# Four small-vector loads queued behind the eighth token tile's load, sinks loaded as whole rows

## The chip, the cores and the metric

The kernel runs on one core of one Trainium2 chip. Times are device microseconds (us) of one execution; the number that counts is the median over several executions. A profile comes from one execution of its own, and its span runs from that execution's first recorded instruction to its last.

The engines are TensorE (PE; its weight loads are PEld), VectorE (DVE), ScalarE (ACT), GpSimd (POOL) and SyncE (SP). SP computes nothing here: it issues plain loads and stores. POOL issues the transfers that add to what lies at their destination. "SPq" marks a DMA-issuing instruction on SP's queue.

## What is computed

One layer of a hybrid encoder block on x, 1024 tokens by 1024 channels, float32:

```
h    = rmsnorm(x, norm_g)
proj = h @ w_in                    # q, k, v, za, u, vs, zs, two merge gates
a    = window_sink_attention(rope(q), rope(k), v, att_sinks)   # 16 heads of 64
a    = (a * silu(za)) @ w_att_out
v2   = layernorm(gelu(vs), sg_ln_g, sg_ln_b)
sg   = gelu(u) * (masked sg_w per 128-token block @ v2 + sg_b)
sg   = (sg * silu(zs)) @ w_sg_out
y    = sigmoid(gate_a + b_merge[0]) * a + sigmoid(gate_s + b_merge[1]) * sg
out  = rmsnorm(x + y @ w_o, final_g)
```

The small vectors of this case are `att_sinks` (16 numbers, one per head), `b_merge` (2 x 1024, laid out 128 x 16), `sg_ln_g` and `sg_ln_b` (1024 each, laid out 128 x 8).

## The kernel before, in words

**Products.** Every float32 product is made of three products of a high and a low part in TensorE's fp32r format: high by high, high by low, low by high. `split` (L170 on) makes a high part with an ACT cast (L177) and a low part with a DVE subtraction (L178). The large products take two row blocks and two column blocks at a time and use seven block products in the place of eight (`gemm_pair`, `product` at L396).

**The head** is the first stage, to about 101 us. Tokens come in eight tiles of 128 rows. `normed_tile(t)` (L669) does for tile t, in this order: `load_x(t)` (L571, the DMA at L575) into one of the three `wr` buffers that `raw_tile` (L94) hands out in turn; `scale_of` (L633): an ACT Square of the tile with its row sums (L648), then the inverse root, made of one ACT Sqrt (L148) and four small DVE instructions (L150 to L155); `scaled_part` (L651): for each half of 512 channels one DVE scaling in place (L654) and four TensorE transposes into a PSUM bank (L659); `cast_part` (L663): an ACT cast to the high part (L665) and a DVE subtraction to the low part (L666); and an ACT copy of the transposed half (L678). The second transposes of a tile are the last readers of its `wr` buffer, so they free it. Tiles 0, 1 and 2 are loaded and normalised in `first_tiles` (L743). Then a loop runs (L842):

```python
for t in range(5):
    if t > 1:
        vs_gemm(t)
    if t + 3 < NT:
        normed_tile(t + 3)
```

`vs_gemm(t)` (L710, products at L682) multiplies tile t by half of the `vs` weights. At t = 3 the loop also calls `of_chain` twice (weights that POOL adds up in place, `s` tiles) and `ask(6)` (L829): a plain load of weight tile 6 into a `wr` buffer. At t = 4 it loads and adds up `apart`, calls `ask(7)`, and `of_raw` (L838) casts and splits what `ask(6)` brought, at L177 and L178. After the loop comes a block whose order on PE, ACT and DVE is written by hand; it begins with four `plain` weights (L901), the third of which is the one of `ask(6)`, the fourth that of `ask(7)`.

The buffers decide when a load can be issued. Tile 3 takes tile 0's `wr` buffer, tile 4 that of tile 1, and so on: tile 5 waits for tile 2, tile 6 for tile 3, `ask(6)` for tile 4, tile 7 for tile 5, `ask(7)` for tile 6.

**Order of instructions.** Outside the hand-ordered blocks a scheduler orders each engine's instructions when the program is built. Each engine then runs its own list strictly in that order, and an instruction that waits holds up all those behind it on its engine. `after(second, first)` (L180) only puts `second` behind `first` in an engine's list; it adds no wait at run time. SP's transfers go to one hardware queue, POOL's to another.

**Small vectors.** The sinks are loaded by two DMAs of 64 partitions (L1028), 4 runs of 2 numbers (8 bytes) in each partition, so that head pair c of parity e lies in columns 2c and 2c+1 of the half e; both stand behind tile 4's load in SP's list. `bm_sb`, `lg_sb` and `lb_sb` are loaded by L1032 to L1034 with no order given. `nsink_sb` is the negated `sink_sb` (L1139). First readers: `lb_sb` and `lg_sb` at 112.8 and 115.0 us (L1092, L1111), `sink_sb` at 189.5 (L1139), `bm_sb` at 680.7 (L1910).

Of the kernel before, what the change touches and what calls it, by code (L numbers as in the profile page):

```python
# [25 lines left out]
F32 = mybir.dt.float32  # L26
# [6 lines left out]
P = 128  # L33
# [4 lines left out]
NT = S // P  # L38
# [16 lines left out]
def hybrid_tile(  # L55
# [16 lines left out]
    nc = tc.nc  # L72

    dram = ctx.enter_context(tc.tile_pool(name="dram", bufs=1, space=bass.MemoryType.DRAM))
    const = ctx.enter_context(tc.tile_pool(name="const", bufs=1))
# [5 lines left out]
    def nm(s):  # L81
        count[0] += 1
        return f"{s}_{count[0]}"
# [4 lines left out]
    def mtile(shape, dt, tag, bufs, pool=None):  # L88
        return (pool or main).tile(shape, dt, name=nm(tag), tag=tag, bufs=bufs)
# [4 lines left out]
    def raw_tile():  # L94
        return mtile([P, D], F32, "wr", 3)
# [20 lines left out]
    make_identity(nc, ident[:])  # L116
    warm = const.tile([P, 1], F32, name="warm")

    sink_sb = const.tile([P, 8], F32, name="sink_sb")
    nsink_sb = const.tile([P, 8], F32, name="nsink_sb")  # L120
    bm_sb = const.tile([P, 16], F32, name="bm_sb")
    lg_sb = const.tile([P, KC], F32, name="lg_sb")
    lb_sb = const.tile([P, KC], F32, name="lb_sb")
# [56 lines left out]
    def after(second, first):  # L180

        tc.add_manual_dep(
            second.ins,
            first.ins.name,
            mybir.DependencyInfo(mybir.DependencyClass.NoSync, mybir.DependencyReason.DATA),
            reason="order",
        )
# [5 lines left out]
    def slot(name, shape=(P, 4, HALF), dt=F32R):  # L193

        return mtile(list(shape), dt, "T_" + name, 1)

    def new_b(names=FORMS):
        return {n: (slot(n + "h"), slot(n + "l")) for n in names}
# [26 lines left out]
    def add_to(dst, src):  # L225
        return nc.gpsimd.dma_start(dst, src, accum_op=ALU.add)

    def copy_to(dst, src):
        nc.sync.dma_start(dst, src)
# [150 lines left out]
    term = [None]  # L380
# [188 lines left out]
    x_loads = {}  # L569

    def load_x(t, parts=1):  # L571
        xt = raw_tile()
        for c in range(parts):
            cs = slice(c * D // parts, (c + 1) * D // parts)
            x_loads[t] = nc.sync.dma_start(xt[:, cs], x[t * P : (t + 1) * P, cs])  # L575
        return xt
# [8 lines left out]
    x_in = {0: load_x(0, 2)}  # L585
# [7 lines left out]
    def keep_busy(n):  # L593
        return [
            nc.tensor.matmul(idle[:], ones_b[:, 0:P], ones_b[:], start=True, stop=True) for _ in range(n)
        ]
# [3 lines left out]
    behind = keep_busy(7)[-1]  # L600
    for j in range(4):
        for i in range(2):
# [8 lines left out]
            behind = spread  # L611
# [7 lines left out]
    f = {n: slot(at, dt=F32) for n, at in (("f11", "t3l"), ("f21", "t4l"))}  # L619
# [13 lines left out]
    def scale_of(t, vector=False):  # L633
        xt = x_in[t] if t in x_in else load_x(t)
        if t == 0:
            s0, s1, base, half_base = (stat() for _ in range(4))
            for c, ss in enumerate((s0, s1)):
                nc.scalar.activation(junk[:, half_of(c)], xt[:, half_of(c)], AF.Square, accum_out=ss[:])
            nc.vector.tensor_scalar(base[:], s0[:], 1.0 / D, EPS, op0=ALU.mult, op1=ALU.add)
            nc.vector.tensor_scalar_mul(half_base[:], base[:], -0.5)  # L640
            return xt, rstd_of(s1[:], 1.0 / D, (base[:], half_base[:]))
        ss = stat()
        if vector:
            squares[t] = nc.vector.scalar_tensor_tensor(
                junk[:], xt[:], 1.0, xt[:], op0=ALU.mult, op1=ALU.mult, accum_out=ss[:]
            )
        else:
            squares[t] = nc.scalar.activation(junk[:], xt[:], AF.Square, accum_out=ss[:])  # L648
        return xt, rstd_of(ss[:], 1.0 / D)

    def scaled_part(t, j, xt, r):  # L651
        cs = half_of(j)
        gain = g_in[j][:] if t < 2 else g_sb[:, cs]
        scale = nc.vector.scalar_tensor_tensor(xt[:, cs], xt[:, cs], r[:], gain, op0=ALU.mult, op1=ALU.mult)  # L654
        scalings.append(scale)
        pt = bank("o" if t == 1 else "tp")
        for i in range(4):
            k = j * 4 + i
            turn = nc.tensor.transpose(pt[:, i * P : (i + 1) * P], xt[:, k * P : (k + 1) * P], ident[:])  # L659
        p3 = pt[:].rearrange("p (k c) -> p k c", k=4)  # L660
        return p3, (f[f"f{j + 1}{t // 4 + 1}"][:, :, tokens(t)], p3), scale, turn

    def cast_part(t, j, p3):  # L663
        hi, lo = quarter_of(t, j)
        casts.append(nc.scalar.copy(hi, p3))  # L665
        los.append(nc.vector.tensor_sub(lo, p3, hi.bitcast(F32)))  # L666
        return casts[-1], los[-1]

    def normed_tile(t, scale=None):  # L669
        xt, r = scale or scale_of(t)  # L670
        if t == 4:
            hb.update(new_b(("b22",)))
            f.update((n, slot(at, dt=F32)) for n, at in (("f12", "t4h"), ("f22", "t3h")))
        for j in range(2):
            p3, copy, _, _ = scaled_part(t, j, xt, r)
            if t <= 4 or j:
                cast_part(t, j, p3)
            nc.scalar.copy(*copy)  # L678
# [31 lines left out]
    def vs_gemm(t, middle=None):  # L710

        acc = vs_acc[t] = bank("o" if t in (2, 3) else "mm")[:]
        part = acc
        if t == 1:
            vs_acc["p1"] = bank("sc")[:]
        dst = xh[:, t, 0:HALF]
        for k in range(KC):
            if middle and k in middle:
                middle[k]()
            if t < 4 and k == 4:  # L720
                nc.scalar.copy(dst, acc)
                part = vs_acc["p1"]
            pace[0] = vs_step(part, t, k, *vs_w[k], (0, KC - 1) if t == 4 else (k & 4, k | 3))
            if t == 4 and k in (0, 4):
                part_of_early(1)
        if t == 4:
            nc.scalar.copy(dst, acc)
        else:
            nc.vector.tensor_add(dst, dst, part)
# [91 lines left out]
    def of_chain(c, nxt=None):  # L821
        raw = chain[c] if c < 2 else apart
        weights.append(vs_weights(raw[:]))
        if nxt is not None:
            add_to(raw[:], w[W_VS + nxt])
# [3 lines left out]
    def ask(first, second=None, raw=None):  # L829
        raw = raw or raw_tile()  # L830
        copy_to(raw[:], w[W_VS + first])
        if second is not None:
            add_to(raw[:], w[W_VS + second])
        waiting.append(raw)
# [3 lines left out]
    def of_raw():  # L838
        weights.append(vs_weights(waiting.pop(0)[:]))

    first_tiles()
    for t in range(5):  # L842
        if t > 1:
            vs_gemm(t)
        if t + 3 < NT:
            normed_tile(t + 3)
        if t == 2:
            for c in range(2):
                chain.append(mtile([P, D], F32, "s", 2))
                copy_to(chain[c][:], w[W_VS + 4 + c])  # L850
        if t == 3:
            for c in range(2):
                of_chain(c, 6 + c)
            ask(6)
        if t == 4:
            copy_to(apart[:], w[W_VS + 4])
            add_to(apart[:], w[W_VS + 6])
            add_to(apart[:], w[W_VS])
            ask(7)
            of_raw()  # L860
# [162 lines left out]
    for t in (0, 4):  # L1023
        nc.vector.tensor_scalar_mul(mv[:, t, 1:2], mv[:, t, 1:2], 1.0 / D)
    nc.vector.tensor_scalar_mul(mv[:, 5:8, 1], mv[:, 5:8, 1], 1.0 / D)
    sinks_by = sinks.rearrange("(c e r) -> e c r", e=2, r=2)
    for e in range(2):
        later = nc.sync.dma_start(  # L1028
            sink_sb[e * 64 : (e + 1) * 64].rearrange("p (c r) -> p c r", r=2), sinks_by[e].partition_broadcast(64)
        )  # L1030
        after(later, x_loads[4])
    nc.sync.dma_start(bm_sb[:], b_merge)  # L1032
    nc.sync.dma_start(lg_sb[:], ln_g)
    nc.sync.dma_start(lb_sb[:], ln_b)  # L1034
    split_next()
    head.close()

# [98 lines left out]
    while late:  # L1136
        late.pop(0)()
    stage.close()
    after(nc.vector.tensor_scalar_mul(nsink_sb[:], sink_sb[:], -1.0), term[0])  # L1139


    stage = ExitStack()
# [622 lines left out]
    with tc.manual_schedule(engines={mybir.EngineType.PE, mybir.EngineType.Activation, mybir.EngineType.DVE}):  # L1765
        p = 0
# [297 lines left out]
    for p in range(4):  # L2064
        n, t, acc, x11 = N_PAIRS + p, T_ORDER[p], accs[p], firsts[p]
# [204 lines left out]
```

## Time and profile before

| | us |
|---|---|
| three runs: lowest, median, highest | 907.41, 909.19, 909.72 |
| the profiled execution, its time | 906.95 |
| its span | 905.2 |
| PE busy / DVE busy / ACT busy / POOL busy | 890.8 / 700.1 / 547.9 / 152.8 |
| granted TensorE clock, mean | 0.999 |

The profile has a page of totals and answers to questions on single engines, lines and stretches of time. In an answer in order of time, a row gives the start and the length in us, the engine, the line, the operation, what it writes and reads, and how many instructions are merged (x2); a bracket at the end gives how long the engine stood idle ahead of it, and what released it. In the table by stretches, each engine's busy time stands in turn (PE, PEld, DVE, ACT, POOL), then the granted clock, the mean busy share of the 16 DMA engines, and the rate in GB/s.

### The profile page before, as it was taken

Reading aid. Unit: us, or ns where it says so; the run is one execution under the profiler, and the core shown is the slowest. Engines: PE = TensorE matmul, PEld = TensorE weight load, DVE = VectorE, ACT = ScalarE, POOL = GpSimd, SP = SyncE. Lnnn points to the kernel's source line nnn. Section 1 sums busy time; section 2 is a strip of 40 time slices with the busy share of each in tenths; the row PEclk is TensorE's granted clock in tenths of the full one; section 3 lists DMA queues with packets and bytes.
Section 4 is the critical chain, followed back from the end, with each engine's and each line's share of the span. In section 5 each row is a group of like instructions: output and inputs, shape, how many; then the busy total and the mean of one; then the engine's idle time right before and its main releaser. Section 6 shows DMA issues by size and latency. Waiting matters only on the chain.

```text
span 905.2 us, 13294 instructions
## 1 busy us (share of the span) xinstructions
PE 890.8 (98%) x4269; PEld 742.3 (82%) x4269; DVE 700.1 (77%) x1256; ACT 547.9 (61%) x1098; POOL 152.8 (17%) x230
## 2 busy tenths in 40 slices
PE   8899999999999999999999999999999999999997
PEld 5678888888888888888888888888888888888886
DVE  6788876666678677888888887656698699579986
ACT  8677733334445567888778886444476385367443
POOL 2112322213011001222211111011100111210012
PEclk9999999999999999999999999999999999999999
DMA  7888998867788879999998996875568665998633
GB/s 279 210 209 196 267 191 178 178 153 232 240 276 261 276 260 321 287 249 269 250 351 266 251 236 185 302 268 185 166 211 307 216 204 177 283 323 284 204 111 122
DMA packets 131765, 213.45 MB, mean 236 GB/s; under 512 B 12940, under 2 KB 61072, under 8 KB 131696
## 3 DMA queue, kind: packets, MB, share of 16 engines
q1 hardware_dynamic: 108728, 148.89, 50.6%
q0 software_dynamic: 22672, 63.45, 29.7%
q8 instruction: 34, 0.56, 0.2%
q10 hardware_dynamic: 296, 0.27, 0.1%
q14 instruction: 35, 0.29, 0.1%
HBM read 155.80 MB, written 90.31 MB: 272 GB/s over the span
## 4 chain that ended last, share of the span: by engine, by line
PE 94%; DMA 2%; ACT 2%; DVE 1%; issue 0%; SPq 0%; ACTq 0%
PE ps_mm L396 45%; PE ps_o L396 27%; PE ps_tp L396 4%; PE ps_sc L1451 3%; PE ps_sc L396 2%; DMA wr<-in_x_dram 2%; PE ps_o L682 2%; PE ps_tp L1103 2%; PE ps_tp L1532 2%; PE ps_o L1592 2%; PE ps_mm L682 2%; PE ps_tp L682 1%; PE ps_sc L682 1%; PE ps_o L1600 1%; PE ps_tp L1542 1%; ACT wl L648 1%
## 5 line engine op out<-in xcount | busy, mean ns | idle before, releaser
L177 ACT CAST wh<-s 128x1024 fp32r<-128x1024 f32 (+1 forms) x84 | 84.4, 1006 | 78.2 <-PE ps_mm L396 27.6
L178 DVE TENSOR_TENSOR wl<-s,wh 128x1024 fp32r<-128x1024 f32 (+1 forms) x84 | 98.5, 1173 | 18.6 <-ACT wh L177 18.2
L178 DVE TENSOR_TENSOR wl<-wr,wh 128x512 fp32r<-128x512 f32 (+1 forms) x65 | 61.6, 949 | 63.2 <-ACT wh L177 61.3
L177 ACT CAST wh<-wr 128x512 fp32r<-128x512 f32 (+1 forms) x65 | 53.9, 831 | 63.8 <-PE ps_mm L396 36.3
L1492 ACT ACTIVATE pr<-ps_sc,sm 128x192 f32<-128x192 f32 (+2 forms) x128 | 51.3, 408 | 24.6 <-DVE sm L1483 21.4
L396 PE MATMUL ps_o<-T_b22h,wh 128*128 128x512 f32 x148 | 59.1, 399 | 0.0
L339 POOL DMA_DIRECT2D sums<-in_w_dram x48 | 35.5, 888 | 133.8 <-PE ps_mm L396 83.1
L396 PE MATMUL ps_o<-T_t1h,wh 128*128 128x512 f32 x148 | 58.1, 392 | 0.0
L396 PE MATMUL ps_o<-T_b22h,wl 128*128 128x512 f32 x148 | 57.9, 391 | 0.0
L396 PE MATMUL ps_o<-T_t1h,wl 128*128 128x512 f32 x148 | 57.8, 390 | 0.0
L396 PE MATMUL ps_o<-T_b22l,wh 128*128 128x512 f32 x148 | 57.8, 390 | 0.0
L396 PE MATMUL ps_o<-T_t1l,wh 128*128 128x512 f32 x148 | 57.7, 390 | 0.0
L396 PE MATMUL ps_mm<-T_t4h,wh 128*128 128x512 f32 (+1 forms) x144 | 55.9, 388 | 0.0
L396 PE MATMUL ps_mm<-T_t2h,wh 128*128 128x512 f32 x140 | 55.4, 396 | 0.0
L396 PE MATMUL ps_mm<-T_t4h,wl 128*128 128x512 f32 (+1 forms) x144 | 55.3, 384 | 0.0
L396 PE MATMUL ps_mm<-T_t4l,wh 128*128 128x512 f32 (+1 forms) x144 | 55.3, 384 | 0.0
L396 PE MATMUL ps_mm<-T_b11h,wh 128*128 128x512 f32 x140 | 55.2, 394 | 0.0
L396 PE MATMUL ps_mm<-T_t3h,wh 128*128 128x512 f32 x140 | 54.9, 392 | 0.0
L396 PE MATMUL ps_mm<-T_b11l,wh 128*128 128x512 f32 x140 | 54.7, 391 | 0.0
L396 PE MATMUL ps_mm<-T_b11h,wl 128*128 128x512 f32 x140 | 54.6, 390 | 0.0
L396 PE MATMUL ps_mm<-T_t3h,wl 128*128 128x512 f32 x140 | 54.6, 390 | 0.0
L396 PE MATMUL ps_mm<-T_t2h,wl 128*128 128x512 f32 x140 | 54.6, 390 | 0.0
(488 smaller groups left out, 2476.5 us busy)
## 6 DMA issues: line engine op xcount, KB each, us to landing
wr<-in_w_dram SPq DMA_DIRECT2D x80, 256.0 KB
sums<-in_w_dram POOLq DMA_DIRECT2D x24, 512.0 KB, 7.6
s<-sums SPq DMA_DIRECT2D x24, 512.0 KB
wr<-in_w_dram SPq DMA_DIRECT2D x17, 512.0 KB
q_hl<-qhl SPq DMA_DIRECT2D x16, 512.0 KB
q<-q_hl SPq DMA_DIRECT2D x64, 128.0 KB
y_dr<-x POOLq DMA_DIRECT2D x28, 256.0 KB, 6.3
sums<-in_w_dram POOLq DMA_DIRECT2D x24, 256.0 KB, 8.1
```

The source lines that it names most:

```text
L177: hi_casts.append(nc.scalar.copy(hi, src))
L178: return nc.vector.tensor_sub(lo, src, hi.bitcast(F32))
L339: return lambda: paced(nc.gpsimd.dma_start(dst, src, accum_op=op))
L396: mm = nc.tensor.matmul(acc, lt, rt, start=fresh and k == 0 and n == 0, stop=k == 3 and n == 2, skip_group_check=True,)
L648: squares[t] = nc.scalar.activation(junk[:], xt[:], AF.Square, accum_out=ss[:])
L682: mm = nc.tensor.matmul(acc, lt, rt, start=first and n == 0, stop=last and n == 2, skip_group_check=True)
L1103: nc.tensor.matmul(pm[:, t * P : (t + 1) * P], xh[:, half * 4 + t, g * P : (g + 1) * P], bias[-1][1][:, g % 2, :], start=True, stop=True,)
L1451: nc.tensor.matmul(sc[:, i, lo:hi], q_of[:, c, i * P : (i + 1) * P], kt[:, f, lo:hi], start=f == 0, stop=f == 1,)
L1492: nc.scalar.activation(st.pr[:, i, place_of(c, lo, hi)], st.sc[c][:, i, lo:hi], AF.Exp, bias=st.nmax[:, c, i : i + 1], scale=-1.0, accum_o ...
L1532: nc.tensor.transpose(st.inner[0:wide, at : at + P], st.pr[:, i, place_of(c, 64 if st.t else P, 192)], ident[:])
L1542: nc.tensor.transpose(st.ends[0:wide, i * P : (i + 1) * P], st.pr[:, i, P : P + wide], ident[:])
L1592: nc.tensor.matmul(st.po[:], lt, rt, start=i == 0, stop=False, skip_group_check=True)
```

## The change

Three edits.

1. At the end of the loop's pass t = 3, behind `normed_tile(6)` and ahead of `of_chain` and `ask(6)`, tile 7 is loaded. It so takes the buffer that tile 4 leaves, `ask(6)` takes tile 5's and `ask(7)` still tile 6's.
2. The four small loads are issued there too, in one chain behind tile 7's load on SP's list: `lb_sb`, `lg_sb`, `bm_sb`, `sink_rows`.
3. The sinks come as one DMA of whole rows, all 16 numbers (64 bytes) to each of 128 partitions. At the place of the old negation, three DVE copies sort them by parity: one for each half of the partitions into a scratch tile, one back; the fourth DVE instruction negates.

```diff
-    sink_sb = const.tile([P, 8], F32, name="sink_sb")
-    nsink_sb = const.tile([P, 8], F32, name="nsink_sb")
+    sink_rows = const.tile([P, 16], F32, name="sink_rows")
+    sink_sb, nsink_sb = sink_rows[:, 0:8], sink_rows[:, 8:16]
...
         if t + 3 < NT:
             normed_tile(t + 3)
+        if t == 3:
+            x_in[7] = load_x(7)
+            behind = x_loads[7]
+            for dst, src in (
+                (lb_sb, ln_b),
+                (lg_sb, ln_g),
+                (bm_sb, b_merge),
+                (sink_rows, sinks.partition_broadcast(P)),
+            ):
+                later = nc.sync.dma_start(dst[:], src)
+                after(later, behind)
+                behind = later
...
-    sinks_by = sinks.rearrange("(c e r) -> e c r", e=2, r=2)
-    for e in range(2):
-        later = nc.sync.dma_start(
-            sink_sb[e * 64 : (e + 1) * 64].rearrange("p (c r) -> p c r", r=2), sinks_by[e].partition_broadcast(64)
-        )
-        after(later, x_loads[4])
-    nc.sync.dma_start(bm_sb[:], b_merge)
-    nc.sync.dma_start(lg_sb[:], ln_g)
-    nc.sync.dma_start(lb_sb[:], ln_b)
...
-    after(nc.vector.tensor_scalar_mul(nsink_sb[:], sink_sb[:], -1.0), term[0])
+    by_half = mtile([P, NT], F32, f"st{NT}", 5)
+    behind = term[0]
+    for e in range(2):
+        half = slice(e * 64, (e + 1) * 64)
+        by_e = sink_rows[half].rearrange("p (c e r) -> p c e r", e=2, r=2)[:, :, e, :]
+        taken = nc.vector.tensor_copy(by_half[half].rearrange("p (c r) -> p c r", r=2), by_e)
+        after(taken, behind)
+        behind = taken
+    nc.vector.tensor_copy(sink_sb, by_half[:])
+    nc.vector.tensor_scalar_mul(nsink_sb, by_half[:], -1.0)
```

## The prediction, on record before the result

> **What bounds the kernel now.** I read the page first, then who makes TensorE wait, then the stretches, then the lists of the engines where it waits.
>
> ```profile
> span 905.2 us, 13294 instructions
> PE 890.8 (98%) x4269; PEld 742.3 (82%) x4269; DVE 700.1 (77%) x1256; ACT 547.9 (61%) x1098; POOL 152.8 (17%) x230
> ```
> ```profile
> PE ps_tp L659 <- DVE wr L654: 2.2, 1, 2.2
> PE ps_tp L659 <- ACT xh L727: 1.6, 1, 1.6
> PE ps_o L595 <- DVE T_b22l L106: 1.5, 1, 1.5
> PE ps_tp L659 <- issue: 0.9, 1, 0.9
> PE ps_sc L603 <- DVE wh L589: 0.9, 1, 0.9
> PE ps_mm L777 <- ACT T_t2h L700: 0.5, 1, 0.5
> ```
> ```profile
> 0.00:50.00 50.00, 42.22 (x203) 31.30 (x203) 35.84 (x78) 36.40 (x69) 10.15 (x21) 1.00 0.81 248
> 50.00:100.00 50.00, 50.00 (x224) 41.43 (x223) 40.35 (x55) 38.49 (x60) 10.52 (x17) 1.00 0.84 214
> ```
>
> TensorE is the bound. The second fence holds all its waits of the whole execution, and all lie in the head: from 50 to 100 us it is busy for 50.00 of 50.00. So whatever lets TensorE through the first 50 us sooner arrives at the end, as long as nothing behind starts to wait. Three of the waits stand at L659, the transposes of token tiles 5, 6 and 7:
>
> ```profile
> 36.97 0.63 PE L659 MATMUL ps_tp<-ident,wr 128*128 128x128 f32 x4 [2.21 <-DVE wr L654]
> 43.29 0.63 PE L659 MATMUL ps_tp<-ident,wr 128*128 128x128 f32 x4 [0.91 <-issue]
> 49.40 0.63 PE L659 MATMUL ps_tp<-ident,wr 128*128 128x128 f32 x4 [1.57 <-ACT xh L727]
> ```
>
> 2.21 + 0.91 + 1.57 = 4.69 us: all that this change can win on TensorE. (The bracket names the last releaser only; the lists below show what held it.) What feeds these tiles is SP's list:
>
> ```profile
> 10.65 0.43 SPq L1032 DMA_DIRECT2D bm_sb<-in_b_merge_dram  x1
> 11.33 0.33 SPq L1033 DMA_DIRECT2D lg_sb<-in_ln_g_dram  x1
> ...
> 17.63 0.33 SPq L575 DMA_DIRECT2D wr<-in_x_dram  x1
> 18.00 1.41 SPq L1028 DMA_DIRECT2D sink_sb<-in_sinks_dram  x2
> 19.46 0.60 SPq L1034 DMA_DIRECT2D lb_sb<-in_ln_b_dram  x1
> 21.27 0.33 SPq L575 DMA_DIRECT2D wr<-in_x_dram  x1
> ```
> ```profile
> 31.63 0.33 SPq L229 DMA_DIRECT2D wr<-in_w_dram  x1
> 38.34 0.33 SPq L575 DMA_DIRECT2D wr<-in_x_dram  x1
> 44.70 2.47 SPq L229 DMA_DIRECT2D wr<-in_w_dram  x2
> ```
> ```profile
> 21.27 10.50 DMA wr<-in_x_dram
> ...
> 38.34 6.04 DMA wr<-in_x_dram
> ```
> ```profile
> 20.00:23.00 3.00, 3.00 (x19) 2.64 (x18) 1.97 (x6) 3.00 (x7) 0.35 (x1) 1.00 0.16 52
> 23.00:26.00 3.00, 3.00 (x15) 2.23 (x14) 2.92 (x5) 3.00 (x7) 0.00 (x0) 1.00 0.27 38
> ```
>
> Tile 4 is asked for at 17.63, tile 5 at 21.27; 31.63 is `ask(6)`, 38.34 tile 7, 44.70 `ask(7)`. Tiles 5 and 7 have the same size, yet tile 5 takes 10.50 us to land and tile 7 takes 6.04. While tile 5 is under way the DMA engines are nearly idle: shares of 0.16 and 0.27. It is not short of bandwidth; it stands in SP's queue behind the sinks, whose 512 pieces of 8 bytes drain slowly, and behind `lb_sb`. ScalarE and VectorE show the rest:
>
> ```profile
> 28.84 0.59 ACT L678 COPY T_t4l<-ps_tp 128x512 f32<-128x512 f32 x1
> 31.79 1.06 ACT L648 ACTIVATE wl<-wr 128x1024 f32<-128x1024 f32 x1 [2.36 <-DMA wr<-in_x_dram]
> ...
> 36.10 1.07 ACT L648 ACTIVATE wl<-wr 128x1024 f32<-128x1024 f32 x1
> ...
> 38.31 1.05 ACT L177 CAST wh<-wr 128x1024 fp32r<-128x1024 f32 x1 [1.04 <-DMA wr<-in_w_dram]
> 39.27 0.58 ACT L678 COPY T_t4h<-ps_tp 128x512 f32<-128x512 f32 x1
> ...
> 40.22 0.30 ACT L148 ACTIVATE st<-st,eps_sb 128x1 f32<-128x1 f32 x1
> ...
> 44.41 1.06 ACT L648 ACTIVATE wl<-wr 128x1024 f32<-128x1024 f32 x1 [2.61 <-DMA wr<-in_x_dram]
> ```
>
> The Squares of tiles 5, 6 and 7 are at 31.79, 36.10 and 44.41. At 38.31 stands the cast of `ask(6)`. It comes ahead of two things that tile 6 needs: the copy of tile 5's half at 39.27 (VectorE works behind it) and tile 6's own root at 40.22. So tile 6's transposes, at 43.29, are held by the landing of a weight that is only multiplied later.
>
> **The change part by part.**
>
> *The early small loads go* (bm, lg, sinks, lb). Tile 5's issue does not move: it waits for tile 2's buffer, not for SP. It should land well inside the 6.04 us of tile 7, at 27.3 or before, ahead of the end of ScalarE's work at 28.84 + 0.59 = 29.43. Its Square then starts at 29.43 instead of 31.79, 2.36 us earlier, and its transposes can start at 36.97 - 2.36 = 34.61. TensorE runs dry at 36.97 - 2.21 = 34.76. **The wait of 2.21 goes.** What is late next is tile 6.
>
> *Tile 7 ahead of `ask(6)`.* It takes tile 4's buffer, so SP issues it at 31.63, where `ask(6)` is now; `ask(6)` moves to tile 5's release. Does tile 7 land sooner than `ask(6)` did, 38.31 - 31.63 = 6.7 us later? POOL's adds fill the engines at that time:
>
> ```profile
> 30.96 0.88 POOL L226 DMA_DIRECT2D apart<-in_w_dram  x1 [10.61 <-DMA apart<-in_w_dram]
> 31.53 2.07 POOL L226 DMA_DIRECT2D s<-in_w_dram  x2
> ```
> ```profile
> 32.00:38.00 6.00, 3.79 (x22) 2.95 (x21) 3.89 (x9) 4.90 (x10) 1.60 (x2) 1.00 0.95 203
> 38.00:42.00 4.00, 4.00 (x21) 3.31 (x19) 2.09 (x6) 2.80 (x5) 0.77 (x1) 1.00 1.05 213
> ```
>
> The engines are 0.95 busy while `ask(6)` lands. Tile 6's data is out of the queue sooner now, and POOL's adds start somewhat earlier, so I take 0 to 1 us off: tile 7 lands at 37.3 to 38.3, and I use 37.8. The Trainium skill, DMA: Bandwidth & Descriptors, Issuing engines are not separate DMA queues, says that transfers started by different engines run on the same 16 DMA engines and interleave; it speaks against gaining by asking earlier, and the two shares above agree with it.
>
> Now the wait that the change adds. Tile 7's Square is ready in ScalarE's list where the cast of `ask(6)` was: same buffer, same size, same moment of issue, and it comes from earlier in the program than the cast. I expect it in that place, behind tile 6's Square and ahead of the copy of tile 5's half. ScalarE then waits there for tile 7 as it waits now for the weight; behind it are tile 5's copies and cast and tile 6's root, and behind these VectorE's subtractions and scaling, and TensorE. The Square and its read of the sums take 0.1 us more than the cast (1.16 against 1.05). So tile 6's transposes start at 43.29 - 0.5 + 0.1 = 42.9. TensorE reaches them 2.2 us sooner than now, and waits about 2.7 us in the place of 0.91: **most of what tile 5 gave is taken back here.**
>
> *Tile 7's own wait of 1.57* goes. Its Square is done 5 us ahead of now, and the list between tile 6 and tile 7 on TensorE is the same work: 49.40 - 1.57 - 43.29 = 4.54 us from tile 6, so tile 7 starts at 42.9 + 4.54 = 47.4 in the place of 49.40.
>
> *`ask(6)` and `ask(7)` come later in the list.* `ask(6)` is issued when tile 5's transposes end, near 36.0, behind four small loads. It changes places with tile 7, whose data landed at 44.4 when asked for at 38.34; I take 42 to 45. Its cast then stands where tile 7's Square is now, ahead of the copies of tile 6's transposes, and tile 7's transposes wait for these, since they write the same PSUM banks. From landing to tile 7 that is 1.05 + 0.58 = 1.7 us if VectorE has scaled tile 7 by then, and about 4.5 if its list keeps tile 7's scaling behind tile 6's work as now (44.41 to 49.40, less a half us for the Square's sums). A landing at 42 costs nothing by either; one at 45 costs nothing by the first and 2 us by the second. I take 43 and the second: 43 + 4.5 = 47.5, 0.1 later than the 47.4 above. The multiplication itself, the third `plain` weight, follows two others and does not come into it before 50.
>
> *The small loads behind tile 7.* 512 pieces again, but of 32 and 64 bytes. No row shows this load alone; from below nothing (hidden under POOL's adds), from above the delay of the old group, 10.50 - 6.04 = 4.5 us on the transfer behind it, `ask(6)`. I take 2 us, inside the 42 to 45 above, because half the pieces are the bm and lg loads, which held up nothing that waited. Their readers come at 112 us and later.
>
> ```profile
> 189.50 0.16 DVE L1139 TENSOR_SCALAR nsink_sb<-sink_sb 128x8 f32<-128x8 f32 x1
> ...
> 196.78 0.69 DVE L283 TENSOR_TENSOR s<-wr 128x512 f32<-128x512 f32 x1 [5.09 <-DMA wr<-in_w_dram]
> ```
>
> *The sorting.* Three DVE instructions more, each like L1139's 0.16: 0.5 us at 189.5. TensorE does not wait there, and VectorE stands idle for 5.09 us soon after; cost nothing. Without that cover it would be 0.5.
>
> **Sum.** Transposes of tile 7 at 47.5 in the place of 49.40: **1.9 us gained**, 4.69 of waits becoming about 2.8. The profiled execution would go from 906.95 to 905.05, its span from 905.2 to 903.3. The median shown, 909.19, lies 2.24 above the profiled execution; from it I forecast 909.19 - 1.9 = **907.3 us**.
>
> **The rivals.**
>
> *All three waits go: 904.5.* Tile 7's Square does not hold tile 6, either because the scheduler puts it behind tile 5's copies and tile 6's root, or because tile 7 lands by 35. Then 4.69 is gained. For it: tile 5's half is transposed by 35.3, close to where ScalarE falls idle, so a small shift in the order suffices. Against it: the cast stands there today under the same conditions. The Trainium skill, DMA: Bandwidth & Descriptors, Anatomy of one DMA, gives about 2.0 us plus the bytes by 436 GB/s for one transfer; as an estimate that is 3.2 us for 512 KB, a landing at 34.8, and so this rival's time. The trace disagrees: 10.50 and 6.04 for that size.
>
> *The small loads hold `ask(6)`, slower: 912.7.* If they drain behind tile 7 as the old sinks did ahead of tile 5, and beside POOL's adds, `ask(6)` lands at 44 + 4.5 = 48.5. By the longer way above tile 7's transposes follow at 48.5 + 4.5 = 53.0, 3.5 us behind the 49.40 of now. From a landing of 43 on this eats the gain, and from 44.9 on the change loses. Against it: there are no pieces of 8 bytes any more.
>
> *No change: 909.2.* The lists fall differently: the tiles' transposes placed earlier among TensorE's products wait just as long, or `ask(6)` lands near 45.
>
> **How the numbers follow.** Forecast 0.5; all waits gone 0.25; no change 0.13; slower 0.12. The range, 903.9 to 910.0, holds the first three with a half us of scatter around them and leaves out the slower one. What a measurement of this kernel can tell from no change is about 0.3%, 2.7 us. Faster by more than that is the second case and the upper tail of the first: 0.36. Slower by more: 0.12. Within: 0.52.
>
> **What would show each step.** Right: ScalarE's Square of tile 5 directly behind the work ending at 29.4 with no wait for a DMA; DMA shares near 0.2 between 20 and 26 gone; no wait at tile 5's transposes, one of 2 to 3.5 us at tile 6's, none at tile 7's; a Square waiting for `in_x` just ahead of tile 5's copies. Wrong: tile 6's transposes before 41; a wait at `plain` weights between 46 and 60; any wait of TensorE after 60, where I have taken it that every load has time to spare.

## The result, and the profile after

| | before | changed |
|---|---|---|
| median, lowest to highest (5 runs each, side by side) | 909.72 (907.41 to 910.33) | **905.07** (904.32 to 905.66) |
| the profiled execution, its time and span | 906.95, 905.2 | 904.32, 902.5 |
| mean granted clock in it | 0.999 | 0.998 |
| TensorE's waits at L659, tiles 5, 6 and 7 | 2.21 + 0.91 + 1.57 | 0 + 1.30 + 0.96 + 0 |

The ratio is 0.9953, with a 95% interval of 0.9938 to 0.9967: faster by 0.3 to 0.6%. The page's totals after:

```profile
span 902.5 us, 13292 instructions
PE 890.4 (99%) x4269; PEld 742.5 (82%) x4269; DVE 700.3 (78%) x1259; ACT 547.5 (61%) x1098; POOL 152.7 (17%) x230
```

Every engine does what it did, three DVE instructions apart; the span lost 2.7 us, 2.4 of them waits of TensorE at L659. The first rows of the table of waits:

```profile
PE ps_o L595 <- DVE T_b22l L106: 1.5, 1, 1.5
PE ps_tp L659 <- issue: 1.3, 1, 1.3
PE ps_tp L659 <- DVE st L153: 1.0, 1, 1.0
```

TensorE's list in order of time, the transposes of tile 5, of tile 6 in two halves, and of tile 7 (x8):

```profile
34.95 0.63 PE L659 MATMUL ps_tp<-ident,wr 128*128 128x128 f32 x4
...
39.17 0.63 PE L659 MATMUL ps_tp<-ident,wr 128*128 128x128 f32 x4 [1.30 <-issue]
42.14 0.63 PE L659 MATMUL ps_tp<-ident,wr 128*128 128x128 f32 x4 [0.96 <-DVE st L153]
46.03 1.03 PE L659 MATMUL ps_tp<-ident,wr 128*128 128x128 f32 x8
```

Tiles 5 and 7 no longer wait, tile 6 waits twice. Why it does stands in ScalarE's list:

```profile
29.36 1.07 ACT L648 ACTIVATE wl<-wr 128x1024 f32<-128x1024 f32 x1
...
35.63 1.06 ACT L648 ACTIVATE wl<-wr 128x1024 f32<-128x1024 f32 x1 [1.50 <-DMA wr<-in_x_dram]
36.59 0.19 ACT L648 ACTIVATION_READ_ACCUMULATOR wl<-wr 128x1 f32 x1
36.81 0.29 ACT L148 ACTIVATE st<-st,eps_sb 128x1 f32<-128x1 f32 x1
37.01 0.56 ACT L678 COPY T_t4h<-ps_tp 128x512 f32<-128x512 f32 x1
38.99 1.06 ACT L648 ACTIVATE wl<-wr 128x1024 f32<-128x1024 f32 x1 [1.41 <-DMA wr<-in_x_dram]
39.96 0.19 ACT L648 ACTIVATION_READ_ACCUMULATOR wl<-wr 128x1 f32 x1
40.05 0.57 ACT L665 CAST T_b22h<-ps_tp 128x512 fp32r<-128x512 f32 x1
...
41.37 0.58 ACT L678 COPY T_t3h<-ps_tp 128x512 f32<-128x512 f32 x1
41.86 1.05 ACT L177 CAST wh<-wr 128x1024 fp32r<-128x1024 f32 x1
```
```profile
40.65 0.69 DVE L666 TENSOR_TENSOR T_b22l<-ps_tp,T_b22h 128x512 fp32r<-128x512 f32 x1 [0.98 <-ACT T_b22h L665]
41.26 0.74 DVE L654 SCALAR_TENSOR_TENSOR wr<-wr,st,g_sb 128x512 f32<-128x512 f32 x1
```

Tile 5's Square runs at 29.36 without a wait. Tile 6's Square, at 35.63, now waits 1.50 us for its own data: that is tile 6's first wait. Tile 7's Square, at 38.99, waits 1.41 us in front of the cast of tile 5's second half at 40.05. Two things that tile 6's second half needs stand behind that cast: on VectorE the subtraction that reads its result (40.65) and then the scaling of that half (41.26 to 42.00), and on ScalarE the copy at 41.37 that empties the PSUM bank into which that half is transposed. Both end just ahead of 42.14: the second wait. The cast of `ask(6)`, at 41.86, waits for nothing.

Tile 6 lands later than the queue in front of it would explain. The DMA engines by stretches, and POOL's adds:

```profile
20.00:23.00 3.00, 3.00 (x19) 2.63 (x18) 1.99 (x6) 3.00 (x7) 0.33 (x1) 1.00 0.80 141
23.00:26.00 3.00, 3.00 (x15) 2.22 (x13) 2.88 (x6) 3.00 (x6) 0.99 (x2) 1.00 0.82 246
```
```profile
25.01 0.88 POOL L226 DMA_DIRECT2D apart<-in_w_dram  x1 [4.69 <-DMA apart<-in_w_dram]
25.58 1.19 POOL L226 DMA_DIRECT2D s<-in_w_dram  x1
28.18 0.85 POOL L226 DMA_DIRECT2D s<-in_w_dram  x1 [1.41 <-ACT T_b21h L665]
```

Where the engines stood at 0.16 and 0.27 they are at 0.80 and 0.82: nothing clogs the queue. But the adds were held by that clog too, though they go by POOL's queue: before, the second add to `apart` waited 10.61 us for the first one to land, now 4.69. They came at 30.96 and 31.53 before and come at 25.01 to 28.18 now, beside the loads of tiles 6 and 7.

**The scatter before.** Executions of the kernel before differ among themselves by over 6 us (906.09 to 912.56), those of the changed one by less than 2. A further look at the kernel before, told among the experiments, shows another form of the same head, with one wait of 4.52 us at tile 6 and, behind it, TensorE at half its clock. Over the 83 executions of the kernel before that ran beside the experiments, 18 had a mean granted clock of 0.998 or more (median 906.92), 30 had 0.996 or 0.997 (908.45) and 35 had 0.995 or less (910.10). The changed kernel had 0.997 or more in all ten. So two things make up the gain in the median: fewer waits in like executions (2.63 us in the pair of profiles, about 2 us between the medians at a clock of 0.998 or more), and no executions of the longer form among the ten. Why `ask(6)` lands so much later in one execution than in another stays open.

### The profile page after: what moved, and what is told of

It reads as the page before. It is cut to its first block, busy times and chain, and to the rows that moved or that the text cites. A ratio compares the mean times of both kernels' runs of the same rounds, so it can differ in the third digit from the quotient of the medians.

```text
span 902.5 us, 13292 instructions
## 1 busy us (share of the span) xinstructions
PE 890.4 (99%) x4269; PEld 742.5 (82%) x4269; DVE 700.3 (78%) x1259; ACT 547.5 (61%) x1098; POOL 152.7 (17%) x230
## 4 chain that ended last, share of the span: by engine, by line
PE 97%; DMA 1%; ACT 1%; DVE 0%; SPq 0%; issue 0%; ACTq 0%
PE ps_mm L396 45%; PE ps_o L396 27%; PE ps_tp L396 4%; PE ps_sc L1463 3%; PE ps_sc L396 2%; PE ps_o L682 2%; PE ps_mm L682 2%; PE ps_sc L682 2%; PE ps_tp L1106 2%; PE ps_tp L1544 2%; PE ps_o L1604 2%; PE ps_tp L682 1%; PE ps_o L1612 1%; DMA wr<-in_x_dram 1%; PE ps_tp L1554 1%; DMA T_t3h<-in_w_dram 1%
```

## The experiments

Each gives its median beside runs of the kernel before on the same chip; that kernel's medians were 908.65, 909.61 and 908.37 us in the three sets, so the ratio compares better than the time.

### The changed kernel again

No edit, beside the first set.

> The changed kernel again, beside the three variants. Theory G (given back): tile 5's wait is gone, but POOL's adds start 6 us sooner, lie beside tiles 6 and 7 and hold their landing, so that about half of the 4.69 us of waits is kept: 2.3 to 2.7 us under the kernel before by the profiles; by the medians anything from 2.3 to 4.7. Rival S (sum of the parts): both parts add up, 4 us or more in every comparison.

904.9 us (904.21 to 905.26), ratio 0.9960 [0.9947, 0.9973]. Tile 6 waits 0.73 + 1.41 us, tiles 5 and 7 none. The gain holds: 3.6 us by the ratio, 3.75 between the medians, which fits theory G and is under the 4 us of S.

### The small loads late, tile 7 where it was

From the changed kernel (the calls of `of_chain` and `ask(6)` only move up; their old lines below, which go, are not shown):

```diff
         if t == 3:
-            x_in[7] = load_x(7)
+            for c in range(2):
+                of_chain(c, 6 + c)
+            ask(6)
+        if t == 4:
             behind = x_loads[7]
             for dst, src in (
```

> The small loads moved late and the sinks in whole rows, but tile 7 still asked for behind ask(6). G: tile 5's transposes near 34.9 with no wait to speak of, tile 6's Square waits for its data until about 35.6, the cast of ask(6) until about 39, tile 6's transposes near 44, tile 7's near 48.5 in the place of 49.40: about 0.9 us gained. S: 2.2 us gained, tile 5's whole wait.

908.44 us, ratio 0.9996 [0.9985, 1.0008]: **nothing is gained**, less than either theory said. Tile 5's wait is gone, its transposes run at 34.67. But see ScalarE, TensorE, and two stretches by windows, whose third last number is the granted clock:

```profile
40.19 1.04 ACT L177 CAST wh<-wr 128x1024 fp32r<-128x1024 f32 x1 [5.21 <-DMA wr<-in_w_dram]
```
```profile
45.16 1.09 PE L659 MATMUL ps_tp<-ident,wr 128*128 128x128 f32 x4 [5.06 <-ACT st L148]
```
```profile
42.00:45.00 3.00, 0.00 (x0) 0.00 (x0) 2.89 (x9) 2.29 (x6) 0.00 (x0) 0.64 0.06 23
45.00:50.00 5.00, 4.84 (x16) 4.14 (x17) 4.34 (x11) 1.79 (x4) 0.72 (x1) 0.53 0.28 71
```

`ask(6)` was issued at 31.50 beside adds that now came at 26.34 and 26.91. ScalarE waits 5.21 us for it, in front of tile 5's copies, and TensorE waits 5.06 us at tile 6, more than the three waits of before together (4.69). Behind it the granted clock is 0.53. The same list from tile 6's first transposes to the first `plain` product takes 50.48 - 45.16 = 5.32 us here, and 46.53 - 43.29 = 3.24 in the profile of before: 2.1 us more for the clock.

### Tile 7 first, the small loads where they were

From the kernel before:

```diff
+        if t == 3:
+            x_in[7] = load_x(7)
```

> Tile 7 asked for ahead of ask(6), the small loads as before. G: tile 5 still lands 10.5 us after its issue and its wait of 2.2 us stays; the waits at tiles 6 and 7 shrink to under 0.7 together: 1.8 to 2.5 us gained, as much as the whole change within 0.6 us. S: no more than 1.5 us gained, and at least 1 us less than the whole change.

906.89 us, ratio 0.9987 [0.9975, 0.9998]: 1.2 us gained by the ratio, 1.8 between the medians. That is well under the whole change, as theory S said. The waits in its profile:

```profile
36.69 0.63 PE L659 MATMUL ps_tp<-ident,wr 128*128 128x128 f32 x4 [1.79 <-DVE wr L654]
...
47.49 0.63 PE L659 MATMUL ps_tp<-ident,wr 128*128 128x128 f32 x4 [1.68 <-DVE wr L654]
```
```profile
44.44 1.05 ACT L177 CAST wh<-wr 128x1024 fp32r<-128x1024 f32 x1 [3.26 <-DMA wr<-in_w_dram]
```

Tile 5 waits nearly as before. Tile 6 waits for nothing. The cast of `ask(6)` lands late, ahead of tile 6's copies, and costs 1.68 us at tile 7's second half.

### The sinks as whole rows at their old place

From the kernel before, edit 3 alone (the sorting is as in the change and not shown):

```diff
-    for e in range(2):
-        later = nc.sync.dma_start(
-            sink_sb[e * 64 : (e + 1) * 64].rearrange("p (c r) -> p c r", r=2), sinks_by[e].partition_broadcast(64)
-        )
-        after(later, x_loads[4])
+    later = nc.sync.dma_start(sink_rows[:], sinks.partition_broadcast(P))
+    after(later, x_loads[4])
```

> The kernel before with the sinks as one load of whole rows, sorted later, but issued at the old place behind tile 4, and the other small loads where they were. Theory F (form: pieces of 8 bytes drain slowly): tile 5 lands by 29.4, its Square waits for no DMA and its transposes start by 35.0; the total then behaves like the variant with late small loads, no more than 1 us under the kernel before, since the cast of ask(6) holds tile 6. Rival P (place: any small load there holds tile 5): tile 5's Square still starts at 31 or later.

908.56 us, ratio 0.9997 [0.9983, 1.0012]. Tile 5's Square does not wait any more, so it was the pieces of 8 bytes and not the place that held tile 5. And again nothing is gained, by the same way as with the small loads late:

```profile
41.17 1.04 ACT L177 CAST wh<-wr 128x1024 fp32r<-128x1024 f32 x1 [2.68 <-DMA wr<-in_w_dram]
```
```profile
46.15 1.08 PE L659 MATMUL ps_tp<-ident,wr 128*128 128x128 f32 x4 [4.95 <-ACT st L148]
```

### The sinks' loads issued twice

From the kernel before, a second pair of the same loads into `nsink_sb`, which is overwritten later:

```diff
+    for dst in (sink_sb, nsink_sb):
...
+                dst[e * 64 : (e + 1) * 64].rearrange("p (c r) -> p c r", r=2), sinks_by[e].partition_broadcast(64)
```

> The kernel before, the sinks' two loads issued twice (the second copy is overwritten later). Theory F: twice 512 pieces of 8 bytes; tile 5 lands about 7 us later than now, 17 to 18 us behind its issue; the wait at its transposes grows from 2.2 to 8 to 10 us, and the clock is halved behind it in every execution: 6 to 11 us slower than the kernel before. If the pieces cost nothing: no difference within 1 us.

909.06 us, ratio 1.0005 [0.9991, 1.0019]: no slower, so theory F missed by far. Tile 5's Square waits 3.43 us. With 512 pieces it waited 2.36, 1.96 and 0.83 in three profiles (the one of before, the one with tile 7 first, and the second look below). So 512 more pieces cost some 1 to 2.6 us of that wait and not 7. One more thing moves here: `lb_sb`'s load, ahead of tile 5's before, now stands behind it. How the clog grows with the number of pieces, and what sets its length, stays open.

### A second look at the kernel before

No edit.

> The kernel before again, for its profile. If the mean granted clock is under 0.998, its timeline has a half-clock stretch of 3.4 or 6.8 us that begins within the waits at the transposes of tiles 5 to 7; if it is 0.998 or more, none there.

910.21 us, mean clock 0.994.

```profile
46.41 1.09 PE L659 MATMUL ps_tp<-ident,wr 128*128 128x128 f32 x4 [4.52 <-issue]
```
```profile
41.44 1.05 ACT L177 CAST wh<-wr 128x1024 fp32r<-128x1024 f32 x1 [4.75 <-DMA wr<-in_w_dram]
```
```profile
45.00:50.00 5.00, 3.59 (x13) 3.15 (x14) 4.31 (x10) 2.62 (x5) 0.72 (x1) 0.50 0.06 20
```

Here tile 5 waits only 0.78 us, and the late landing of `ask(6)` costs 4.52 at tile 6 with the clock at 0.50 behind, as expected at this mean clock. The same cast is in the same place as in the profile that I predicted from, where it waited 1.04.

### The adds held back

From the changed kernel, the adds to `s` made to wait for tile 6's Square, and the second add to `apart` for tile 7's; a real wait this time (`held_until(move, first)` makes `move` wait at run time until `first` is done):

```diff
-            add_to(raw[:], w[W_VS + nxt])
+            added = add_to(raw[:], w[W_VS + nxt])
+            if 6 in squares and 7 not in squares:
+                held_until(added, squares[6])
...
-            add_to(apart[:], w[W_VS])
+            held_until(add_to(apart[:], w[W_VS]), squares[7])
```

> The changed kernel, with POOL's adds to the chain tiles held until tile 6's Square and the second add to apart until tile 7's. G: tile 6 lands by 32 and tile 7 by 36; the waits at their transposes fall from 2.26 us to under 0.6: 1.7 to 2.3 us faster than the changed kernel. S, or if another traffic delays tile 6: no difference within 0.5 us. Slower if the chain tiles come too late for their casts at 52.6 and 55.6.

906.26 us, ratio 0.9973 [0.9963, 0.9983]: not faster than the changed kernel (0.9960), where theory G expected 1.7 to 2.3 us. But the Squares of tiles 6 and 7 run at 34.80 and 36.80 with no wait for data: it was the adds that made tiles 6 and 7 late. Then the adds, at 36.27 and 39.63, meet `ask(6)`:

```profile
43.90 1.05 ACT L177 CAST wh<-wr 128x1024 fp32r<-128x1024 f32 x1 [3.76 <-DMA wr<-in_w_dram]
```
```profile
46.95 0.76 PE L667 MATMUL ps_tp<-ident,wr 128*128 128x128 f32 x4 [2.15 <-DVE wr L662]
```

### The adds held until the weight is cast

From the changed kernel, the same three adds made to wait for the cast of `ask(6)`.

```diff
-                of_chain(c, 6 + c)
+                of_chain(c)
...
-            add_to(apart[:], w[W_VS])
...
+            for c in range(2):
+                held_until(add_to(chain[c][:], w[W_VS + 6 + c]), hi_casts[-1])
+            held_until(add_to(apart[:], w[W_VS]), hi_casts[-1])
```

> The changed kernel with POOL's adds to the chain tiles and the second one to apart held until the cast of ask(6). Theory G: tiles 6, 7 and ask(6) each land beside little other traffic, the Squares and the cast wait for nothing, all waits at the transposes together under 0.5 us, no half-clock stretch in the head: 1.8 to 2.3 us faster than the changed kernel. If the chain tiles now come too late, waits appear between 52 and 62 and it is no faster.

906.18 us, ratio 0.9969 [0.9956, 0.9983]: again no faster than the changed kernel. No transposes wait, and tile 7's run at 44.09, 1.9 us ahead of the changed kernel's. That is lost again between 65 and 76 us, later than expected, where products wait, most of them for weights that the adds make (the last row is another wait):

```profile
PE ps_mm L690 <- DVE wl L178: 1.5, 2, 0.8
...
PE ps_mm L690 <- ACT wh L177: 0.4, 1, 0.4
PE ps_mm L690 <- ACT xh L960: 0.3, 1, 0.3
```

### The wait filled with products

From the kernel with the small loads late and tile 7 at its old place; the tiles' transposes are pinned near where they stood:

```diff
+        if t == 4:
+            for _ in range(4):
+                nc.tensor.matmul(acc, ident[:], g_sb[:, 0:HALF], start=True, stop=True)
...
+            if t == 4 and k == 3:
+                after(turns[6], pace[0])
...
+                if (c, t, k) == (0, 0, 0):
+                    after(turns[7], pace[0])
```

> The kernel with the small loads late and tile 7 at its old place (e1, 908.44 us), with four extra float32 products of the identity by the gains (128x512) put on TensorE ahead of the t = 4 products, and the transposes of tiles 6 and 7 pinned within two or three products of where they stood. They write a PSUM bank that the next product overwrites, so nothing that is computed changes. By the transposes' 0.16 us for 128 columns they take 2.6 to 3.4 us, inside the 5.06 us that TensorE waits at tile 6 there: the wait becomes about 2, and TensorE arrives at the same moment. Theory C (what e1 lost beyond its waits is the half clock that follows a wait of about 5 us): the stretch at half clock from 42.83 to 49.66 goes, the mean clock is 0.996 or more in nearly all executions, and the median falls by about 2.2 us (half of the 4.5 us that the stretch reaches beyond the wait), to 906.2. Theory W (only the waits count, the clock rows are a side show): 908.4 or a little more, whatever the clock rows show.

```profile
37.65 3.60 PE L723 MATMUL ps_mm<-g_sb,ident 128*128 128x512 f32 x8
...
44.65 1.33 PE L661 MATMUL ps_tp<-ident,wr 128*128 128x128 f32 x8 [0.67 <-ACT st L148]
```

The clock behaves as theory C said: 0.998 or more in ten of twelve executions, 0.996 and 0.997 in two, where the kernel without the filling never reached 0.998. The time does not: 907.92 us, ratio 0.9996 [0.9982, 1.0009], no different from the 0.9996 without it. By the medians theory W is the nearer one. TensorE still reaches tile 6 as late as the data lets it. In executions with a shorter wait the filling may cost time of its own; the runs don't part the two. So the half clock follows from the wait, but how much of the median it makes, and how much the lateness of tile 6, is not shown.

### Tile 7's Square behind tile 5's copies

From the changed kernel, the first rival of the prediction made by hand (`copies[t]` is tile t's last copy at L678):

```diff
             squares[t] = nc.scalar.activation(junk[:], xt[:], AF.Square, accum_out=ss[:])
+            if t == 7:
+                after(squares[t], copies[5])
```

> The changed kernel (904.9) with tile 7's Square ordered behind the second copy of tile 5 in ScalarE's list; nothing else. This is the prediction's first rival made by hand. Theory P (the Square that waits for tile 7 is what holds tile 6's second half): the waits of 0.96 to 1.41 us at tile 6's second half go, the 1.30 or 0.73 at its first half stays, since that one hangs on tile 6's own landing, and tile 7 stays without a wait: about 904.0, 1.0 less than the changed kernel. Rival R (tile 7's Square, about 2 us later, makes tile 7's transposes late): as much comes back at tile 7: 904.9.

903.79 us (902.31 to 907.10), ratio 0.9953 [0.9936, 0.9970]. The median is 1.1 us under the changed kernel's 904.9, but that was beside another set; by the ratios (0.9960 and 0.9953 for the changed kernel) the gain is 0 to 0.6 us, inside the intervals. The profile is of the quickest of the eight executions. ScalarE and TensorE:

```profile
39.57 1.07 ACT L648 ACTIVATE wl<-wr 128x1024 f32<-128x1024 f32 x1
```
```profile
38.08 0.63 PE L661 MATMUL ps_tp<-ident,wr 128*128 128x128 f32 x4 [0.58 <-issue]
39.98 0.63 PE L661 MATMUL ps_tp<-ident,wr 128*128 128x128 f32 x4
```

The Square finds its data there, tile 6's second half does not wait, its first half waits 0.58, and tile 7 does not wait. So theory P holds for what waits for what; the 1.0 us that it gave for the time is not shown.

### The adds held, and the cast of the weight out of the way

From the kernel with the adds held until the Squares:

```diff
             of_raw()
+            after(hi_casts[-1], copies[7])
```

> The kernel whose adds are held until the Squares of tiles 6 and 7 (e5, 906.26), with the cast of ask(6) ordered behind tile 7's copies in ScalarE's list. Theory A (the adds decide which landing is late, and a late landing costs only what stands behind it in an engine's list): no wait at the transposes of tiles 5, 6 and 7, no half clock behind them, and next to nothing later (e5 has 0.25 us behind 50 us): the changed kernel's 2.39 us of waits at tiles less 0.3, so about 902.8. Rival B (the third plain weight is cast too late, behind 49 us, and its products wait): one wait of 1 to 3 us between 50 and 56, 904.5 to 906.

903.90 us (903.04 to 904.75), ratio 0.9951 [0.9935, 0.9967]: 2.0 us under the same kernel without the new order by the ratios, 2.4 between the medians. One wait of 0.5 us is left at the tiles, and no `plain` product waits. The time is 1 us above what theory A said. These last two have the lowest medians of the study, but their intervals overlap with that of the changed kernel.

### The sinks' pieces at the new place

From the changed kernel, edits 1 and 2 without edit 3:

```diff
-                (sink_rows, sinks.partition_broadcast(P)),
+                (sink_sb[0:64].rearrange("p (c r) -> p c r", r=2), sinks_by[0].partition_broadcast(64)),
+                (sink_sb[64:128].rearrange("p (c r) -> p c r", r=2), sinks_by[1].partition_broadcast(64)),
```

> The changed kernel (904.9) with the sinks in their old form, two loads of 8-byte pieces, at the new place behind tile 7 and the other small loads; no sorting. It is edits 1 and 2 without edit 3. Theory F (the pieces hold what stands behind them): ask(6) lands 2 to 4.5 us later, its cast holds tile 6's copies and tile 7 waits 1 to 3 us: 906 to 908. Theory G (there, beside the adds, they cost nothing that waits): 904.9 within half a us, and the whole rows bring nothing of their own.

906.34 us, ratio 0.9977 [0.9964, 0.9990]: 1.5 us above the changed kernel by the ratios, though the intervals overlap. Theory F: the pieces of 8 bytes hold `ask(6)`, which was asked for at 37.09.

```profile
40.28 1.06 ACT L649 ACTIVATE wl<-wr 128x1024 f32<-128x1024 f32 x1 [3.30 <-DMA wr<-in_x_dram]
...
47.77 1.05 ACT L178 CAST wh<-wr 128x1024 fp32r<-128x1024 f32 x1 [4.53 <-DMA wr<-in_w_dram]
```
```profile
43.43 0.63 PE L660 MATMUL ps_tp<-ident,wr 128*128 128x128 f32 x4 [2.96 <-DVE st L154]
...
50.83 0.63 PE L660 MATMUL ps_tp<-ident,wr 128*128 128x128 f32 x4 [1.31 <-DVE wr L655]
```

47.77 - 37.09 = 10.7 us to land, where the whole rows let `ask(6)` land within 41.86 - 36.32 = 5.5 (issue and cast of the changed kernel). That costs the 1.31 us. The longer wait, 2.96 us at tile 6, theory F does not explain: there tile 7 lands late (its Square waits 3.30), and its load stands ahead of the pieces. This profile is of the slowest of the twelve executions (908.66).

Edits 1 and 3 without edit 2 (`lb_sb`, `lg_sb` and `bm_sb` left at their old place) were not run, so what moving those three adds is not known.

## Why the prediction was right, and where it was not

The range (903.9 to 910.0) holds 905.07. The forecast of 907.3 was 2.2 us too high: a gain of 1.9 us was forecast and 4.65 came (909.72 to 905.07). The change came out on the side that I gave 0.36, not on the one that I gave 0.52. The range was wide enough to hold that, which is luck more than insight. It is luck too that 905.07 lies near the first rival's 904.5: that rival had all waits go, and 2.26 of 4.69 us are still there. By its steps:

- **TensorE is the bound and its waits in the head are all there is to win: right for the profiled execution.** The span fell by 2.7 us and the waits at tiles from 4.69 to 2.26. In other executions of before there was more to win: 5.3 us of waits at tiles and a stretch at half clock in the second look.
- **The early small loads go: right for tile 5.** Its Square came at 29.36 for my 29.43, its transposes at 34.95 for 34.61. What I missed is that POOL's adds would come 6 us earlier, and make tile 6 late; I had put tile 6's data "out of the queue sooner" to the good. Taking out the clog alone is worth nothing (0.9996 with the small loads late, 0.9997 with the rows alone).
- **Tile 7 ahead of `ask(6)`, and its Square in the place of the cast: the step that failed, in place and in size.** I put the Square ahead of all of tile 5's copies and of tile 6's root, and tile 6 at 42.9 with a wait of 2.7. It stands behind that root and the first copy, and holds the second half only. Tile 6 started at 39.17, which I had named as a sign that I was wrong, and waited 1.30 + 0.96. My first rival was half true: run by hand (tile 7's Square behind the copies) it takes the wait at the second half away, though the gain in time is not clear of the noise. The 3.2 us that I estimated for its landing go by the fit of the Trainium skill, DMA: Bandwidth & Descriptors, Anatomy of one DMA, which holds for transfers that GpSimd issues. Tile 7's load is SP's, and it took 7.28 us in the changed kernel.
- **What this edit is worth was not seen at all.** It takes the cast of `ask(6)` out from in front of tile 6. In the profile that I read this cast waited 1.04 us; in the second look at the kernel before it waits 4.75, and in the kernels with tile 7 at its old place 5.21, 2.68 and, with the sinks loaded twice, nothing. One execution showed me a mild form.
- **Tile 7's own wait goes: right.** Its transposes start at 46.03 without a wait, for my 47.4 to 47.5.
- **`ask(6)` lands at 42 to 45: too late.** Its cast at 41.86 had no wait. The slower rival, a weight held by the small loads, did not come; with the pieces of 8 bytes it does (47.77), so edit 3 is what kept it off; that kernel's ratio is 0.9977 against 0.9960.
- **The sorting costs nothing: right,** by the profile; no wait of TensorE's is near it.
- **The sum.** For the profiled execution I had 905.05 and it took 904.32, 0.7 us off. The other 1.5 us of the 2.2 are in the last step: I added 2.24 us to come from the profiled execution to the median, as if that were a constant. It was 0.75 after the change (905.07 - 904.32). Of the 83 executions of before only 18 had a clock near that of the profiled one (0.998 or more); the 2.24 were the distance to the others, and none of these came in the ten of the changed kernel.

What each edit is worth, by ratio: small loads late as rows, nothing (0.9996); rows alone, nothing (0.9997); tile 7 first alone, 0.13% (0.9987); tile 7 first and the pieces late, 0.23% (0.9977); all three, 0.40 to 0.47% (0.9960, 0.9953). The parts alone do not add up to the whole. As the profiles show it, each takes one late landing away, and the one that is left decides.

## What to carry to other kernels

Ask of every late transfer which instructions stand behind its reader in an in-order list: holding the adds alone only made another landing late (0.9973), and putting that one's reader behind what others need won 2.0 us more (0.9951). When a clogged queue is cleared, everything that it held comes earlier, the traffic that nobody needs yet too, and the next transfer in line may be late instead. One profiled execution can show the mild form of a wait; compare its time with the spread of the runs before adding a constant to it.

## What the runs showed of the hardware

- **Half clock behind a wait.** In 6 of the 14 profiles the trace's clock record shows a stretch at 0.50 in the head, of 3.41 or 6.83 us, that begins in or behind a wait of TensorE: 6.83 with the small loads late (wait 5.06), 3.41 with the adds held (2.15). The Trainium skill, TensorE: Matmul & The Clock Gate, What's actually happening, gives a free-running window of 3413 ns; the lengths agree with one and two of them. It puts the fall to half clock after an idle window of about 3.4 us. Here less was enough, and the length of the wait alone does not decide: a single wait of 2.15 us was followed by half clock, while the 2.21 us in the profile of before were not. In these traces it is how much of the wait falls into one window. In every trace all changes of the clock lie whole multiples of 3.413 us behind its first one, so the windows can be laid out. In each of the 9 windows that half clock followed, TensorE was idle for 2.07 to 2.88 us; in the other 3638 for 1.76 us at most. In the profile of before the edge of a window, at 35.50, cuts the wait in two; with the adds held it lies in one window (PE busy is the first number behind the comma, the clock the third last):

```profile
32.09:35.50 3.41, 2.67 (x12) 1.88 (x10) 2.05 (x6) 3.04 (x7) 1.51 (x2) 1.00 0.89 185
35.50:38.92 3.42, 1.95 (x13) 1.80 (x14) 1.84 (x4) 2.38 (x5) 0.00 (x0) 1.00 1.07 225
```
```profile
43.90:47.31 3.41, 1.26 (x10) 0.92 (x9) 1.85 (x3) 2.65 (x5) 0.00 (x0) 1.00 1.02 324
47.31:50.72 3.41, 3.41 (x11) 2.74 (x10) 2.83 (x4) 2.55 (x4) 0.00 (x0) 0.50 1.05 232
```

  The first change comes at 4.15 to 10.45 us in these traces, so the windows lie elsewhere in each execution, and the same wait can cost half clock in one and not in the next.
- **The same load, 5.5 us or less to 10.7 us.** 512 KB landed within 5.5 us in the changed kernel (`ask(6)`) and after 10.7 behind the sinks' pieces at the new place. With the adds held, tiles 6 and 7 came without a wait (34.80 and 36.80). With the sinks' pieces gone, POOL's add landed sooner too (25.01 for 30.96). So the transfers of SP's and of POOL's queue hold each other up.
- **Small pieces, by their form.** At the old place behind tile 4's load, 512 pieces of 8 bytes made tile 5's Square wait 0.83 to 2.36 us, 1024 of them 3.43; the same numbers as whole rows of 64 bytes, none.
